# S5 stage of a hybrid decoder trunk: input columns in halves, chunk work in pairs, float32 gate products for four blocks

## The chip, the cores and the metric

The kernel runs on one core of a Trainium2 chip. The core has five engines that run at the same time, each with its own queue in order: TensorE (PE in the profile; its weight loads are shown as PEld), VectorE (DVE), ScalarE (ACT), GpSimd (POOL) and SyncE (SP), which here only issues transfers (DMA) between device memory and SBUF. PE writes its results to PSUM. The metric is device time in microseconds of one execution, the median of several runs. All times below are in microseconds where nothing else is said.

## What is computed

Two layers over 256 positions of width 1024; each has a SwiGLU block, a mixer and a second SwiGLU block, all with RMSNorm ahead and a residual sum behind. The mixer of layer 0 is S5, a diagonal state-space layer; that of layer 1 is block-sparse attention. Only S5 bears on this case:

```python
u = (h @ w_in).astype(f32)
...
    bu_re = jnp.einsum('bcgn,gpn->bcgp', u_c, bb_re)
    bu_im = jnp.einsum('bcgn,gpn->bcgp', u_c, bb_im)
    pr, pi, sr, si = lax.associative_scan(combine, (lam_re_b, lam_im_b, bu_re, bu_im), axis=1)
    ...
    y = jnp.einsum('bcgp,gnp->bcgn', st_re, c_re) - jnp.einsum('bcgp,gnp->bcgn', st_im, c_im)
...
y = ys.transpose(1, 0, 2, 3, 4).reshape(bsz, seq, S5_WIDTH) + d_skip.astype(f32) * u
g = jax.nn.gelu(y)
g = g * jax.nn.sigmoid(g @ w_glu.astype(f32))
return g.astype(h.dtype) @ w_out
```

An input product, a complex linear recurrence along the sequence, an output product per group, a gelu, a gate (product with `w_glu`, sigmoid, multiplication) and an output product. The weights of the three large products are 1024 x 1024 each.

## The kernel before

**Split products.** The large products keep nearly the precision of float32 with three fast products: each float32 operand is written as a high and a low part (type float32r), and high x high, high x low and low x high are summed in PSUM. Weights come from device memory as float32 in units of 1024 x 256 or 512 x 512 (`raw`, a ring of three buffers). A half of a unit is split by two instructions: ACT writes `whi` (line 84, or 90 with the norm's gains), DVE writes `wlo` (line 85 or 91). `Stream` keeps the order: `pump` splits the next half if a slot of the nine is free, `get` fetches a half and splits whatever is still missing, `release` gives the slot back after use, and once both halves of a unit are split its `raw` buffer is free and `dmas` issues the next load on SP. Order on every engine is the order in which the program is written out; an instruction that has to wait holds up all that stand behind it on its engine.

**S5.** The 1024 columns are eight blocks of 128. t is one of two halves of 128 positions. The steps, with the lines of the kernel before:

- `w_in` (lines 970 to 976): the input product for 512 columns and one t, 24 matmuls into a `pM` bank; ACT evicts it as `us` with the norm's factor (975), DVE transposes 32 x 32 pieces into `U` (976). Four such passes.
- `t1` (978 to 986), the chunk input of block b: 16 float32 matmuls of `U` with the table `TA` (loaded on SP, line 946). It needs `U` of the block's columns for both t.
- `rot` (988 to 1018), the rotation and scan of a block: on DVE two products `wv` of the PSUM result with the table `TE`, the sum and difference `zi`, two scans `zo`; then on POOL two products `pv` and the sum and difference `hr`. DVE also clears the first columns of `rh` and `zi` each time (993, 1004).
- `y_out` (1034 to 1051), the chunk output: 24 float32 matmuls of `U` and `hr` with the table `TB` (line 954), gelu on ACT (1047), two DVE transposes into `gs` (1050).
- `g_tr` (1053 to 1063): two PE transposes of `gs`; ACT writes the high part (1061), DVE the low part (1062), ACT a float32 copy `gf` (1063).
- `glu` (1065 to 1082): the block's share of the gate product, 24 matmuls of 256 columns into the four banks `pA`.
- `gate` (1084 to 1092): sigmoid on ACT (1087); on DVE the multiplication, the copy to the high part (1091) and the low part.
- `so`, the output product (through `bank_mm` and `mm3`, lines 397 to 399), and `boundary`, which adds the residual and prepares the next stage.

The order is written out by hand at the end of `s5`: rotations 0 to 2 hang as hooks in the third and fourth pass of the input product; after it come chunk outputs, gate products and the remaining chunk inputs by turns, one block at a time, with the gate product three blocks behind the chunk output.

## Time and profile before

| | us |
|---|---|
| median of 3 runs | 993.73 |
| lowest and highest | 992.82, 994.16 |
| profiled execution, its own time | 993.93 |
| its span in the trace | 991.9 |
| PE busy in the span | 973.8 |
| DVE busy | 703.3 |
| ACT busy | 559.2 |
| POOL busy | 192.1 |
| first input product of S5, start | 216.79 |
| first output product of S5, start | 298.30 |

How to read the views that follow. In a list of instructions by time, a row has the start from the begin of the span, the duration, the engine, the line of the kernel, the operation, what is written and read (tile names without numbers), shapes, the count of merged instructions, and in brackets how long the engine had been idle and whose end released it. Matmuls are pipelined: the distance between two starts is the price of one, not its duration. A float32 matmul appears as two records. In a row of groups stand the count, the busy time in all, the mean of one in nanoseconds, and the idle time before them with its releasers. In the view of stretches each row has the stretch, its length, the busy time of PE, PEld, DVE, ACT and POOL with counts, and then the clock granted to PE as a share of full speed, the share of the DMA engines' time and GB/s.

### The profile page before, as it was taken

The numbers are of one execution on the slowest core, as the hardware profiler recorded it, in microseconds if no ns is written. First come the engines' busy times: TensorE is split into PE (matmuls) and PEld (weight loads), VectorE is DVE, ScalarE is ACT, GpSimd is POOL, SyncE is SP. The second block draws the span as 40 slices with busy tenths as digits, with TensorE's granted clock in tenths as the row PEclk, the third lists the DMA queues.
The fourth block names the chain that finished last, engine by engine and source line by source line (L and its number), as shares of the span: only waits on it lengthen the run. The fifth ranks groups of instructions, "written<-read, shape, count | busy, mean of one in ns | idle before, by whom it ended". The sixth has DMA issues, their size and how long they took to land.

```text
span 991.9 us, 17175 instructions
## 1 busy us (share of the span) xinstructions
PE 973.8 (98%) x6695; PEld 866.0 (87%) x6695; DVE 703.3 (71%) x1148; ACT 559.2 (56%) x997; POOL 192.1 (19%) x361
## 2 busy tenths in 40 slices
PE   9999999999799999999999999999999999999998
PEld 7778888888687999999999999998888899999997
DVE  5799777768978776666667766665689667766662
ACT  6646666553255665555545555554898655655540
POOL 4882554414730100000010000000441010000000
PEclk9999999999999999999999999999999999999999
DMA  8978877886656565656536655554445446756531
GB/s 235 277 261 250 293 264 237 301 332 216 236 171 190 193 212 172 211 170 213 170 120 220 216 202 181 194 182 137 131 167 170 157 143 218 248 170 213 170 128 42
DMA packets 140000, 198.71 MB, mean 200 GB/s; under 512 B 18232, under 2 KB 111504, under 8 KB 139664
## 3 DMA queue, kind: packets, MB, share of 16 engines
q1 hardware_dynamic: 133808, 184.32, 56.2%
q0 software_dynamic: 5536, 12.71, 3.6%
q8 instruction: 52, 0.85, 0.4%
q10 hardware_dynamic: 576, 0.61, 0.3%
q14 instruction: 28, 0.23, 0.1%
HBM read 183.89 MB, written 13.66 MB: 199 GB/s over the span
## 4 chain that ended last, share of the span: by engine, by line
PE 84%; DVE 7%; POOL 3%; issue 2%; ACT 2%; DMA 1%; SPq 0%; ACTq 0%; DVEq 0%; POOLq 0%
PE pM L551 12%; PE pM L552 12%; PE pM L553 12%; PE pA L397 9%; PE pA L399 9%; PE pA L398 9%; PE pM L397 5%; PE pM L398 5%; PE pM L399 5%; DVE wlo L85 2%; DVE zo L1010 1%; POOL sc L685 1%; PE pR L331 1%; ACT whi L84 1%; PE pR L861 1%
## 5 line engine op out<-in xcount | busy, mean ns | idle before, releaser
L551 PE MATMUL pM<-xa,whi 128*128 128x256 f32 x1056 | 295.7, 280 | 0.0
L552 PE MATMUL pM<-xa,whi 128*128 128x256 f32 x1056 | 294.9, 279 | 0.0
L553 PE MATMUL pM<-xa,wlo 128*128 128x256 f32 x1056 | 294.7, 279 | 0.0
L91 DVE SCALAR_TENSOR_TENSOR wlo<-raw,gT,whi 128x512 fp32r<-128x512 f32 x328 | 228.2, 748 | 70.5 <-ACT whi L90 70.3
L85 DVE TENSOR_TENSOR wlo<-raw,whi 128x1024 fp32r<-128x1024 f32 (+1 forms) x157 | 191.4, 1234 | 55.6 <-ACT whi L84 54.7
L90 ACT ACTIVATE whi<-raw,gT 128x512 fp32r<-128x512 f32 x328 | 213.7, 711 | 19.6 <-PE pA L399 14.6
L552 PEld LDWEIGHTS pM<-xa,whi 128*128 128x128 f32 x1056 | 198.5, 188 | 2.6
L551 PEld LDWEIGHTS pM<-xa,whi 128*128 128x128 f32 x1056 | 198.5, 188 | 2.3
L553 PEld LDWEIGHTS pM<-xa,wlo 128*128 128x128 f32 x1056 | 198.5, 188 | 0.0
L84 ACT ACTIVATE whi<-raw 128x1024 fp32r<-128x1024 f32 (+1 forms) x157 | 161.1, 1049 | 29.1 <-PE pA L399 8.0
L397 PE MATMUL pA<-whi,ah 128*128 128x512 f32 x352 | 138.8, 394 | 0.0
L398 PE MATMUL pA<-wlo,ah 128*128 128x512 f32 x352 | 137.6, 391 | 0.0
L399 PE MATMUL pA<-whi,al 128*128 128x512 f32 x352 | 137.6, 391 | 0.0
L566 ACT ACTIVATE sg<-gr 128x256 f32<-128x256 f32 x66 | 27.6, 418 | 165.8 <-DVE gr L563 165.8
L397 PE MATMUL pM<-whi,xa 128*128 128x512 f32 x288 | 119.5, 415 | 0.0
L398 PE MATMUL pM<-wlo,xa 128*128 128x512 f32 x288 | 113.1, 393 | 0.1
L399 PE MATMUL pM<-whi,xa 128*128 128x512 f32 x288 | 112.7, 391 | 0.0
L346 POOL TENSOR_TENSOR ms<-ss 128x1 f32<-128x1 f32 x10 | 1.9, 193 | 472.1 <-ACT sq L343 472.1
L399 PEld LDWEIGHTS pA<-whi,al 128*128 128x128 f32 x352 | 66.1, 188 | 14.3
L397 PEld LDWEIGHTS pA<-whi,ah 128*128 128x128 f32 x352 | 66.1, 188 | 11.6
L398 PEld LDWEIGHTS pA<-wlo,ah 128*128 128x128 f32 x352 | 66.2, 188 | 11.3
L563 DVE TENSOR_TENSOR gr<-pM,rrow 128x512 f32<-128x512 f32 x66 | 45.5, 689 | 40.9 <-PE pM L553 40.8
(263 smaller groups left out, 1232.5 us busy)
## 6 DMA issues: line engine op xcount, KB each, us to landing
raw<-in_ffn_w_down_dram SPq DMA_DIRECT2D x44, 1024.0 KB, 5.2
raw<-in_ffn_w_gate_dram SPq DMA_DIRECT2D x80, 512.0 KB, 3.8
raw<-in_ffn_w_up_dram SPq DMA_DIRECT2D x80, 512.0 KB, 4.9
raw<-in_moba_w_qkv_dram SPq DMA_DIRECT2D x12, 1024.0 KB, 5.1
TB<-dB SPq DMA_DIRECT2D x8, 768.0 KB, 6.0
raw<-in_ffn_w_gate_dram SPq DMA_DIRECT2D x16, 256.0 KB, 4.2
raw<-in_ffn_w_up_dram SPq DMA_DIRECT2D x16, 256.0 KB, 4.7
dB<-tt POOLq DMA_DIRECT2D x16, 256.0 KB, 6.0
```

The lines of the kernel that those rows point to most:

```text
L84: nc.scalar.activation(hi[:, c], r[:, c], AF.Copy)
L85: nc.vector.tensor_tensor(lo[:, c], r[:, c], hi[:, c].bitcast(F32), op=OP.subtract)
L90: nc.scalar.activation(hi[:, c], r[:, c], AF.Identity, scale=g)
L91: nc.vector.scalar_tensor_tensor(lo[:, c], r[:, c], g, hi[:, c].bitcast(F32), op0=OP.mult, op1=OP.subtract)
L397: mm(o, xh, wh, start=start, stop=False)
L398: mm(o, xh, wl, start=False, stop=False)
L399: mm(o, xl, wh, start=False, stop=stop)
L551: mm(o, a, xh, start=k == 0 and i == 0, stop=False, skip_group_check=True)
L552: mm(o, a, xl, start=False, stop=False, skip_group_check=True)
L553: mm(o, b, xh, start=False, stop=k == 7, skip_group_check=True)
L563: V.tensor_tensor(gr, ps.rearrange("p (i c) -> p i c", i=2), Rr["row"][:, None, :].to_broadcast([128, 2, 256]), op=OP.mult)
L566: nc.scalar.activation(sg, gr[:, 0, :], AF.Silu)
```

## The change

It edits S5 and what `Stream` needs for it.

- The first 512 input columns are computed in two halves of 256, each for both t (four passes of 24 matmuls of 256 columns instead of two of 512); the second 512 as before. The first half's weights stay in their slots until the fourth pass.
- Chunk inputs go in pairs (`t1x2`), with the loads of two further tables behind them; chunk outputs go in pairs as well. The order at the end of `s5` is written anew: the pair 0, 1 and rotation 0 hang in the third pass, rotation 1 in the fourth, the pair 2, 3 and rotation 2 in the fifth (the first of 512 columns), rotation 3 and the chunk outputs 0 and 1 in the sixth.
- For blocks 0 to 3 (`WHOLE = 4`) the gate product is one float32 matmul instead of three split ones, read from `raw` and `gf` directly. These weights aren't split, and their `raw` buffer is freed when PE has used both halves. `g_tr` then makes no high and low part for these blocks.
- Weights are loaded in another order: three gate units, one output unit, the fourth gate unit, three output units. Where splits are pumped within the gate products is a table, `PUMPS`.
- `rh` and `zi` are cleared once, on POOL; `gs` is made by one DVE transpose instead of two; the gate's copy to the high part is on ACT instead of DVE; the tile of the gate's high and low parts starts at another offset.

```diff
-XO = {'f00': 124, 's5': 124, 'g': 8, 'f01': 80, 'f10': 8, 'moba': 124, 'f11': 8}
+XO = {'f00': 124, 's5': 124, 'g': 124, 'f01': 80, 'f10': 8, 'moba': 124, 'f11': 8}
...
-            self.halves += [(u, 0), (u, 1)]
+            if not units[u][3]:
+                self.halves += [(u, 0), (u, 1)]
...
-        for b in range(4):
-            add(("glu", b), ld_rows(s5_w_glu[0], b * 256))
-        for b in range(4):
-            add(("so", b), ld_rows(s5_w_out[0], b * 256))
+        for key in (('glu', 0), ('glu', 1), ('glu', 2), ('so', 0), ('glu', 3), ('so', 1), ('so', 2), ('so', 3)):
+            w = s5_w_glu if key[0] == "glu" else s5_w_out
+            add(key, ld_rows(w[0], key[1] * 256), whole=key[0] == "glu" and 2 * key[1] < WHOLE)
...
-        def w_in(nh, t, hooks, pumps=(1, 5)):
+        RH = [wp.tile([128, 4, 65], F32, name=f"rh{i}") for i in range(2)]
+        ZI = wp.tile([128, 2, 4, 65], F32, name="zi")
+        for a in RH:
+            P.memset(a[:, :, 0:1], 0.0)
+        P.memset(ZI[:, :, :, 0:1], 0.0)
+
+        def w_in(c0, n, t, hooks, last, pumps=(1, 5)):
...
+                mm3(ps[:, 0:n], X["h"][:, k, ts], X["l"][:, k, ts], wh[:, c:c + n], wl[:, c:c + n], k == 0, k == 7)
+                if k % 2:
+                    if k in pumps:
+                        st.pump()
+                    if last:
+                        st.release(u, (k % 4) // 2)
             us = wp.tile([128, 512], F32, name="us", bufs=1)
-            nc.scalar.activation(us, ps, AF.Identity, scale=Rr[t])
-            V.transpose(U[:, nh * 16:(nh + 1) * 16, t, :], us.rearrange("p (q c) -> p q c", c=32))
+            nc.scalar.activation(us[:, 0:n], ps[:, 0:n], AF.Identity, scale=Rr[t])
+            V.transpose(U[:, c0 // 32:(c0 + n) // 32, t, :], us[:, 0:n].rearrange("p (q c) -> p q c", c=32))
...
+        def t1x2(b):
+            for a in (b, b + 1):
+                t1(a)
+            for a in (b, b + 1):
+                if a + 3 < NB:
+                    ld_a(a + 3)
...
-            for t in range(2):
-                V.transpose(gs[:, t], yg[:, :, t, :])
+            V.transpose(gs, yg.rearrange("p q t c -> p t q c"))
...
-            nc.scalar.activation(GT["h"][:, b, :], ps[:, 0:256], AF.Copy)
-            V.tensor_tensor(GT["l"][:, b, :], ps[:, 0:256], GT["h"][:, b, :].bitcast(F32), op=OP.subtract)
+            if b >= WHOLE:
+                nc.scalar.activation(GT["h"][:, b, :], ps[:, 0:256], AF.Copy)
+                V.tensor_tensor(GT["l"][:, b, :], ps[:, 0:256], GT["h"][:, b, :].bitcast(F32), op=OP.subtract)
...
+                if b < WHOLE:
+                    mm(d, w[:, c], g, start=first, stop=last, skip_group_check=True)
...
-                if o == 7:
+                for _ in range(PUMPS.get((b, o), 0)):
+                    st.pump()
+                if o == 7 and b >= WHOLE:
                     st.release(u, b % 2)
-                if o == 3 and b < 5 or o == 7 and b in (3, 4) or o == 5 and b == 4:
-                    st.pump()
+                elif o == 7 and b % 2:
+                    st.free_raw(u)
...
-            V.tensor_copy(gh, g)
+            nc.scalar.activation(gh, g, AF.Copy)
...
+        PUMPS = {(1, 3): 1, (2, 3): 1, (4, 1): 1, (4, 5): 1, (5, 0): 1, (5, 2): 1, (5, 4): 1, (5, 6): 1}
+        w_in(0, 256, 0, entry_hooks("s5") if entry else {}, False)
+        w_in(0, 256, 1, {}, False, (1,))
+        w_in(256, 256, 0, {5: [lambda: t1x2(0), lambda: rot(0)]}, False, ())
+        w_in(256, 256, 1, {4: [lambda: rot(1)]}, True, (1,))
+        w_in(512, 512, 0, {2: [lambda: t1x2(2), lambda: rot(2)]}, False, ())
+        w_in(512, 512, 1, {1: [lambda: rot(3)], 6: [lambda: y_out(0), lambda: y_out(1)]}, True, ())
+        GT["h"], GT["l"] = home(xp, "g")
+        t1x2(4)
+        rot(4)
         g_tr(0)
+        glu(0)
+        rot(5)
+        g_tr(1)
         y_out(2)
+        y_out(3)
+        glu(1)
+        t1x2(6)
+        rot(6)
+        g_tr(2)
+        glu(2)
+        g_tr(3)
+        rot(7)
+        glu(3)
+        y_out(4)
+        y_out(5)
+        g_tr(4)
+        glu(4)
+        g_tr(5)
+        glu(5)
+        y_out(6)
+        y_out(7)
...
+        g_tr(6)
         g_tr(7)
-        st.pump(2)
         warm(AF.Sigmoid)
-        glu(5)
         for i in range(4):
             glu(6, (2 * i, 2 * i + 1))
             glu(7, (2 * i, 2 * i + 1))
```

64 lines of the change are left out of this document (23 added, 41 removed).

## The prediction

> **What bounds the kernel now.** I read the page first, then busy time by stretch for the S5 part, then the order of instructions on each engine there. The page's span and the chain that ended last:
>
> ```profile
> span 991.9 us, 17175 instructions
> PE 84%; DVE 7%; POOL 3%; issue 2%; ACT 2%; DMA 1%; SPq 0%; ACTq 0%; DVEq 0%; POOLq 0%
> ```
>
> TensorE (PE) carries the chain, so the change is worth what it does to PE's idle time and work. It touches S5 alone, whose stretch runs from the first input product to the first output product. The first and last row below are those two; the three between are PE's long waits (in brackets: idle before, and releaser).
>
> ```profile
> 216.79 0.48 PE L397 MATMUL pM<-whi,xa 128*128 128x512 f32 x1
> ...
> 252.64 0.69 PE L1059 MATMUL pR<-cst,gs 128*128 128x128 f32 x2 [3.97 <-DVE gs L1050]
> ...
> 271.39 0.44 PE L1059 MATMUL pR<-cst,gs 128*128 128x128 f32 x2 [2.28 <-ACT gf L1063]
> ...
> 278.34 0.44 PE L1059 MATMUL pR<-cst,gs 128*128 128x128 f32 x2 [1.95 <-ACT gf L1063]
> ...
> 298.30 0.47 PE L397 MATMUL pA<-whi,xa 128*128 128x512 f32 x1 [0.53 <-DVE xa L1091]
> ```
>
> The stretches around the waits (PE, PEld, DVE, ACT, POOL busy; then granted clock, DMA share, GB/s):
>
> ```profile
> 248.70:252.60 3.90, 0.00 (x0) 0.00 (x0) 3.88 (x6) 0.00 (x0) 2.54 (x4) 1.00 0.63 205
> 252.60:257.00 4.40, 4.36 (x70) 3.75 (x72) 3.83 (x11) 2.13 (x6) 4.03 (x4) 0.61 1.01 407
> ...
> 264.00:272.00 8.00, 5.72 (x102) 5.22 (x98) 7.24 (x13) 1.05 (x3) 6.30 (x6) 1.00 0.54 186
> 272.00:284.00 12.00, 10.05 (x166) 9.38 (x163) 9.19 (x18) 5.34 (x11) 8.39 (x8) 1.00 0.27 89
> ```
>
> While PE waits, VectorE (DVE) is busy: DVE's queue, in order, is what PE waits for. After the idle 3.97 the clock falls to 0.61 for 4.40, a loss of 4.40 x 0.39 = 1.7; after 2.28 and 1.95 it stays at 1.00. So S5 holds 3.97 + 2.28 + 1.95 + 0.53 = 8.7 of idle and 1.7 of slow clock: 10.4 to be won at most.
>
> **The change part by part.** PE prices, each from the distance between starts:
>
> ```profile
> 223.49 0.39 PE L397 MATMUL pM<-whi,xa 128*128 128x512 f32 x1
> ...
> 228.02 0.39 PE L399 MATMUL pM<-whi,xa 128*128 128x512 f32 x1
> ...
> 230.38 1.15 PE L985 MATMUL pA<-U,TA 128*64 128x64 f32 x32
> 231.46 0.50 PE L397 MATMUL pM<-whi,xa 128*128 128x512 f32 x1
> ...
> 244.50 0.34 PE L1043 MATMUL pR<-U,TB 128*64 128x64 f32 x4
> ...
> 247.52 1.15 PE L985 MATMUL pM<-U,TA 128*64 128x64 f32 x32
> ...
> 265.39 0.28 PE L1076 MATMUL pA<-xa,whi 128*128 128x256 f32 x1
> ...
> 267.75 0.28 PE L1078 MATMUL pA<-xa,wlo 128*128 128x256 f32 x1
> ```
>
> ```profile
> 768.36 0.60 PE L1213 MATMUL pA<-kT,qT 128*128 128x256 f32 x2
> 768.79 0.59 PE L1250 MATMUL pR<-pT,vs 128*128 128x256 f32 x2
> ```
>
> A split product of 512 columns takes 4.53/20 = 0.227, one of 256 columns 2.36/20 = 0.118, a float32 one of 256 columns (two records) 0.43, a block's chunk input 1.08, a chunk output (244.50 to 247.52 is two) 1.5.
>
> Input in halves: 96 x 0.118 replace 48 x 0.227: +0.4. Gate products of four blocks: 32 x 0.43 = 13.8 replace 96 x 0.118 = 11.3: +2.4. Chunk inputs in pairs: from 228.02 to 230.38 stand ten products and 0.1 more, the price of a switch; four fewer switches in and out save 0.8. Work in sum: +2.0.
>
> DVE and POOL prices:
>
> ```profile
> 224.42 2.72 DVE L91 SCALAR_TENSOR_TENSOR wlo<-raw,gT,whi 128x512 fp32r<-128x512 f32 x4
> 231.58 0.69 DVE L1005 TENSOR_TENSOR wv<-pA,TE 128x512 f32<-128x512 f32 x1 [0.15 <-PE pA L985]
> 233.58 1.28 DVE L1010 TENSOR_TENSOR_SCAN zo<-rh,zi 128x260 f32<-128x260 f32 x2
> 234.98 0.69 DVE L1005 TENSOR_TENSOR wv<-pA,TE 128x512 f32<-128x512 f32 x1
> 236.30 1.52 DVE L1007 TENSOR_TENSOR zi<-wv,wv 128x256 f32<-128x256 f32 x1
> 238.61 1.82 DVE L1010 TENSOR_TENSOR_SCAN zo<-rh,zi 128x260 f32<-128x260 f32 x2
> ```
>
> ```profile
> 235.00 1.29 POOL L1014 TENSOR_TENSOR pv<-zo,TE 128x512 f32<-128x512 f32 x1 [11.73 <-DVE zo L1010]
> 236.25 1.28 POOL L1015 TENSOR_TENSOR pv<-zo,TE 128x512 f32<-128x512 f32 x1
> 237.61 0.79 POOL L1016 TENSOR_TENSOR hr<-pv,pv 128x256 f32<-128x256 f32 x1
> 238.37 0.92 POOL L1017 TENSOR_TENSOR hr<-pv,pv 128x256 f32<-128x256 f32 x1
> ```
>
> The first rotation (231.58 to 234.86) takes 3.3 with POOL idle; the second (234.98 to 240.43) takes 5.4, its zi standing until POOL's pv ends: the two take turns on their SBUF operands, instruction by instruction. The wv products, which read PSUM, aren't slowed.
>
> ```profile
> L975 ACT ACTIVATE us<-pM,rr 128x512 f32<-128x512 f32 x4 | 2.8, 688 | 15.5 <-PE pM L399 11.9 <-issue 2.3 <-POOL rs_e L307 1.2
> L1063 ACT ACTIVATE gf<-pR 128x256 f32<-128x256 f32 x8 | 3.1, 384 | 20.0 <-DVE xa L1062 20.0
> L976 DVE STREAM_TRANSPOSE U<-us 128x512 f32<-128x512 f32 x4 | 2.8, 700 | 3.2 <-ACT us L975 3.2
> L1062 DVE TENSOR_TENSOR xa<-pR,xa 128x256 fp32r<-128x256 f32 x8 | 3.3, 410 | 0.7 <-ACT xa L1061 0.7
> ```
>
> *The new wait.* The built order puts on DVE: rotation 0, transpose of half two of t = 0, the pair of input-weight splits, rotation 1, transpose of half two of t = 1, rotation 2. PE's chunk input of block 2 reads that last transpose, and behind it on PE stand chunk input 3 and the whole second half of the input product. Count both from the start T of chunk input 0. PE: the pair 2.2, nine products 1.1, the pass 24 x 0.118 = 2.8, six products of 512 at 1.4, switches 0.4: at the wait by T + 7.9. DVE: 1.2 to the rotation (230.38 to 231.58), 3.3, transpose 0.35 (half of 0.70, an estimate), splits 2 x 0.68, rotation 1 at 3.3, transpose 0.35: T + 9.9 with POOL idle. But POOL's work for rotation 0 (about 4.3 from the four rows, 3.0 of it not beside wv) takes turns with just these splits and this rotation; before, it cost rotation 1 2.1. With what PE already needed for block 0 no reason excludes either end: PE idles 9.9 - 7.9 = 2.0 at the least, 2.0 + 3.0 = 5.0 at the most. I take 2.4 for the turns, between the 2.1 seen and the 3.0, since splits now stand in POOL's way as well as zi: an idle of 4.4. That is nearest to the row of 3.97, so the clock drop of 1.7 comes again.
>
> The Trainium skill (TensorE: Matmul & The Clock Gate, "What's actually happening") has the clock halve only after a whole idle window of about 3.4 us, and the windows run free of the kernel. By that an idle of 4.4 covers a whole window three times in ten (an estimate from that page), and the sum would then lose most of the 1.7. The trace agrees that a short idle costs no clock; where the border lies it leaves open, as one idle of 3.97 did drop it.
>
> *Waits that follow.* T itself: the eviction of half one of t = 1 now stands on ACT behind the split of the last input weights, whose load lands late:
>
> ```profile
> 209.49 0.38 SPq L185 DMA_DIRECT2D raw<-in_s_w_in_dram  x1
> raw<-in_s_w_in_dram SPq DMA_DIRECT2D x1, 1024.0 KB, 13.4
> ```
>
> ```profile
> 223.64 2.55 ACT L90 ACTIVATE whi<-raw,gT 128x512 fp32r<-128x512 f32 x4
> ```
>
> 209.5 + 13.4 = 222.9, then two ACT splits at 0.64, an eviction and a transpose of half size (0.35 each) and handovers: 225.4. PE has passed 63 products by 216.8 + 63 x 0.118 + 0.8 for the entering transposes = 225.0: 0.4. Before chunk input 4 PE waits for the last eviction 0.69 and transpose 0.70: 1.4. A gate product right behind its transpose waits for one ACT copy of 0.38 and handovers: 0.5 for blocks 0, 2, 3 (block 1 is covered by two chunk outputs): 1.5. Blocks 4 and 5 still wait for ACT 0.38 and DVE 0.41 one after the other, behind a gelu or two splits: 0.9 each, 1.8. At the end four splits of gate and output weights are pumped within block 5:
>
> ```profile
> 287.68 3.50 DVE L85 TENSOR_TENSOR wlo<-raw,whi 128x1024 fp32r<-128x1024 f32 x3 [0.43 <-ACT whi L84]
> ```
>
> 4 x 1.17 = 4.7 on DVE, begun 1.4 after the block's products, against 2.8 + 2 x 1.5 on PE; both last gelu transposes and their split stand behind them: 1.5 in all.
>
> New waits: 4.4 + 1.7 + 0.4 + 1.4 + 1.5 + 1.8 + 1.5 = 12.7. The sum: 12.7 + 2.0 - 10.4 = +4.3.
>
> Costed at nothing: three memsets on POOL, which has nothing else until rotation 0 but the two small norms; four result splits (0.41) and four weight splits (1.17) that DVE no longer has to make: what they can give is in the 10.4, all of which I credit. The gate's copies go to ACT: one handover more before the first output product, which waits 0.53 for that copy now; PE still has 36 x 0.118 = 4.2 of gate products to run while the first gate is made, and uncovered it costs about that 0.5 once more. The moved address of the gate tile adds no instruction. Chunk tables come in pairs, earlier than their use. Weights of blocks 0 to 3 hold their buffer until PE has used them, so the next loads wait for PE in SP's queue, with the last chunk table behind them: covered if it lands as usual, and a rival below.
>
> The profiled run took 993.93 (span 991.9 and 2.0 around it), 0.2 from the median 993.73. 993.7 + 4.3 = 998.0.
>
> **The rivals.** With S for the idle before chunk input 2, the change is S + (1.7 if the clock drops) - 1.8.
>
> *Not slower: turns with POOL cost nothing at this place.* Then S = 2.0, too short for a drop (2.28 wasn't enough): +0.2, 993.9, no change that could be told. For it: the input splits never ran beside pv in this trace, and rotation 1 could lag POOL and slip between. Against: zi at 1.52 and the scan at 1.82. It decides while S stays under some 2.3; above, each tenth counts fully and the clock comes on top.
>
> *The clock holds through the idle of 4.4:* nothing between 2.28 (held) and 3.97 (dropped) is measured, and one drop may have needed its place in time: 998.0 - 1.7 = 996.3. This is what the Trainium skill's page above would make of it seven times in ten.
>
> *Handovers hide too, faster:* S = 2.0 and of the later waits of 1.4 + 1.5 + 1.8 + 1.5 = 6.2 most, say 4.8, gone, since DVE has eight splits fewer in its queue: 993.9 - 4.8 = 989.1. Against: each of them is a read of what the step before has just made, with no other PE work queued between.
>
> *A late table:* the load for block 7 is issued behind an output-weight load that waits for the fourth gate block.
>
> ```profile
> TB<-dB SPq DMA_DIRECT2D x8, 768.0 KB, 6.0
> ```
>
> From its issue to its use PE has some 10; at 6.0 it is covered, at the 13.4 of the w_in load it is 3.4 late: 1001.4.
>
> **How the numbers follow.** Forecast 998.0, chance 0.45 (own range 996.3 to 1000); clock holds 0.13; POOL costs nothing 0.18; handovers hide 0.12; late table 0.12. Measurement tells 0.2% (2.0) from no change: faster below 991.7 is the handovers' case and a fifth of POOL's, 0.16; 991.7 to 995.7 the rest of POOL's and the low edge of the clock's, 0.19; slower 0.65. The range 991.5 to 1001.5 leaves the handovers' case and half of the late table outside.
>
> **What would show it.** Right: the chunk input of block 2 has an idle of 4 to 5 before it, ended by DVE's transpose U; the clock under 0.7 behind it; rotation 1 over 5; float32 gate products 0.43 apart; the first output product near 302.6. Wrong: S under 2.3, or the first output product before 298.3; a wait on DMA in S5 makes it the last rival.

## The result, and the profile after

The changed kernel takes 997.69 us in the median of 6 runs (996.67 to 998.29); the kernel before takes 993.64 beside it (992.82 to 994.16, 6 runs). The ratio is 1.0039 with a 95% interval of 1.0029 to 1.005: 0.4% slower. The prediction was 998.0. The profiled execution took 997.11, with a span of 995.2.

The page of the changed kernel, its span and the chain that ended last:

```profile
span 995.2 us, 17176 instructions
PE 84%; DVE 6%; POOL 5%; issue 2%; ACT 1%; DMA 1%; SPq 0%; POOLq 0%; ACTq 0%
```

PE still carries the chain with 84%; of the rest, DVE's share went from 7 to 6% and POOL's from 3 to 5%. The instructions of PE in S5 by time (start, duration, operation, in brackets the idle time before and what ended it); the first and last row are the first input and the first output product, as in the prediction:

```profile
216.61 0.36 PE L398 MATMUL pM<-whi,xa 128*128 128x256 f32 x1
...
225.47 2.09 PE L1004 MATMUL pA<-U,TA 128*64 128x64 f32 x64 [0.63 <-issue]
237.16 3.53 PE L1004 MATMUL pA<-U,TA 128*64 128x64 f32 x64 [4.17 <-DVE U L995]
255.17 2.08 PE L1004 MATMUL pM<-U,TA 128*64 128x64 f32 x64 [1.53 <-DVE U L995]
...
258.10 3.72 PE L1091 MATMUL pA<-gf,raw 128*128 128x256 f32 x16 [0.47 <-ACT gf L1072]
261.66 0.38 PE L1067 MATMUL pR<-cst,gs 128*128 128x128 f32 x2
...
283.42 0.38 PE L1093 MATMUL pA<-xa,whi 128*128 128x256 f32 x1 [0.47 <-ACT xa L1070]
...
287.54 0.38 PE L1093 MATMUL pA<-xa,whi 128*128 128x256 f32 x1 [0.47 <-ACT xa L1070]
288.51 0.39 PE L1094 MATMUL pA<-xa,whi 128*128 128x256 f32 x1 [0.59 <-DVE xa L1071]
...
294.89 0.44 PE L1067 MATMUL pR<-cst,gs 128*128 128x128 f32 x2 [0.47 <-DVE gs L1060]
...
302.31 0.39 PE L398 MATMUL pA<-whi,xa 128*128 128x512 f32 x1
```

S5, from the first input product to the first output product, takes 302.31 - 216.61 = 85.70, against 81.51 before: 4.19 more, which is the size of the difference between the medians (997.69 - 993.64 = 4.05). The spans of the two profiled executions differ by less, 995.2 - 991.9 = 3.3: 0.2 is won ahead of S5, and the output product behind it takes 16.36 to the next stage's first transpose instead of 17.07. The three long waits of before (3.97, 2.28, 1.95) are gone. In their place stands one of 4.17, in the middle of the input product, ahead of the chunk input of block 2, and then a row of short ones. The stretches of the long wait and behind it (busy time of PE, PEld, DVE, ACT, POOL; then granted clock, DMA share, GB/s):

```profile
233.00:237.16 4.16, 0.01 (x1) 0.01 (x1) 4.07 (x8) 0.00 (x0) 2.02 (x4) 0.98 0.61 171
237.16:241.60 4.44, 4.44 (x68) 4.25 (x69) 2.39 (x5) 0.00 (x0) 3.66 (x4) 0.64 0.67 214
```

PE does nothing for 4.16, DVE works through all of it, and behind it the clock is at 0.64 for 4.44: a further 4.44 x 0.36 = 1.6. The two chunk inputs that follow the wait take 3.53 for that reason; the pair ahead of it took 2.09. What DVE does in that time, and POOL beside it:

```profile
223.59 1.41 DVE L92 SCALAR_TENSOR_TENSOR wlo<-raw,gT,whi 128x512 fp32r<-128x512 f32 x2 [0.77 <-ACT whi L91]
...
230.20 3.37 DVE L92 SCALAR_TENSOR_TENSOR wlo<-raw,gT,whi 128x512 fp32r<-128x512 f32 x2
233.49 0.68 DVE L1028 TENSOR_TENSOR wv<-pA,TE 128x512 f32<-128x512 f32 x1
...
235.48 1.28 DVE L1033 TENSOR_TENSOR_SCAN zo<-rh,zi 128x260 f32<-128x260 f32 x2
236.68 0.42 DVE L995 STREAM_TRANSPOSE U<-us 128x256 f32<-128x256 f32 x1
```

```profile
230.02 1.30 POOL L1037 TENSOR_TENSOR pv<-zo,TE 128x512 f32<-128x512 f32 x1 [6.95 <-DVE zo L1033]
231.28 1.75 POOL L1038 TENSOR_TENSOR pv<-zo,TE 128x512 f32<-128x512 f32 x1
```

The last row of DVE is the transpose that PE waits for; rotation 1 (233.49 to 236.7) stands ahead of it, and ahead of that the pair of splits, which takes 3.37 beside POOL's two products for rotation 0. The pair of the same shape in the first row, ahead of POOL's products, took 1.41.

### The profile page after: what moved, and what is told of

It reads as the page before. It is cut to its first block, busy times and chain, and to the rows that moved or that the text cites. A ratio compares the mean times of both kernels' runs of the same rounds, so it can differ in the third digit from the quotient of the medians.

```text
span 995.2 us, 17176 instructions
## 1 busy us (share of the span) xinstructions
PE 975.2 (98%) x6711; PEld 868.3 (87%) x6711; DVE 689.3 (69%) x1114; ACT 557.6 (56%) x995; POOL 192.4 (19%) x364
## 4 chain that ended last, share of the span: by engine, by line
PE 84%; DVE 6%; POOL 5%; issue 2%; ACT 1%; DMA 1%; SPq 0%; POOLq 0%; ACTq 0%
PE pM L553 12%; PE pM L552 12%; PE pM L554 12%; PE pA L398 9%; PE pA L400 9%; PE pA L399 9%; PE pM L398 4%; PE pM L399 4%; PE pM L400 4%; DVE wlo L86 2%; PE pA L1091 1%; POOL sc L686 1%; POOL qrs L305 1%; PE pR L1054 1%; PE pR L332 1%
## 5 line engine op out<-in xcount | busy, mean ns | idle before, releaser
L86 DVE TENSOR_TENSOR wlo<-raw,whi 128x1024 fp32r<-128x1024 f32 (+1 forms) x153 | 184.9, 1223 | 55.7 <-ACT whi L85 54.4
L85 ACT ACTIVATE whi<-raw 128x1024 fp32r<-128x1024 f32 (+1 forms) x153 | 156.8, 1049 | 29.2 <-PE pA L400 7.8
L398 PE MATMUL pM<-whi,xa 128*128 128x512 f32 (+1 forms) x304 | 122.0, 401 | 0.0
L399 PE MATMUL pM<-wlo,xa 128*128 128x512 f32 (+1 forms) x304 | 115.7, 381 | 0.3 <-DVE wlo L92 0.2
L400 PE MATMUL pM<-whi,xa 128*128 128x512 f32 (+1 forms) x304 | 115.4, 380 | 0.0
L398 PEld LDWEIGHTS pA<-whi,ah 128*128 128x128 f32 x352 | 66.1, 188 | 11.6
```

Of the source, the lines that this page charges most:

```text
L85: nc.scalar.activation(hi[:, c], r[:, c], AF.Copy)
L86: nc.vector.tensor_tensor(lo[:, c], r[:, c], hi[:, c].bitcast(F32), op=OP.subtract)
L398: mm(o, xh, wh, start=start, stop=False)
L399: mm(o, xh, wl, start=False, stop=False)
L400: mm(o, xl, wh, start=False, stop=stop)
```

## Experiments

Times are medians; each ratio is to the kernel before, run beside it, with a 95% interval. "S5" is the stretch between the two products above, in the profiled execution of each kernel.

**Rotation 1 behind the transpose.** Is the 4.17 the loss, and is it rotation 1's place in DVE's queue?

```diff
-w_in(256, 256, 1, {4: [lambda: rot(1)]}, True, (1,))
-w_in(512, 512, 0, {2: [lambda: t1x2(2), lambda: rot(2)]}, False, ())
+w_in(256, 256, 1, {}, True, (1,))
+w_in(512, 512, 0, {0: [lambda: rot(1)], 2: [lambda: t1x2(2), lambda: rot(2)]}, False, ())
```

> The changed kernel with one move: rotation 1 is issued behind the eviction and transpose of half two of t = 1, so the transpose that the chunk input of block 2 waits for stands ahead of rotation 1 on DVE. Nothing else is changed. Theory (that wait is the loss, and its price is the idle of 4.17 plus the slow clock behind it): DVE is through with the two splits at about 233.6 and makes the transpose at 234.0, so the idle before the chunk input of block 2 falls from 4.17 to about 1.0, the granted clock behind it stays at 0.98 or more, and the time falls by 3.2 + 1.4 = 4.6, to about 993.1. Rival (the wait is only moved): rotation 2, chunk input 4 or the handovers of the gate products take back at least half of it: 995.5 or more, with an idle above 3 before chunk input 4. Rival (the loss is in the float32 gate products): no change, 997.5 or more.

Measured: 992.09, ratio 0.9988 (0.9979 to 0.9996). PE by time, then DVE by time:

```profile
232.79 2.08 PE L1004 MATMUL pA<-U,TA 128*64 128x64 f32 x64 [1.01 <-DVE U L995]
```

```profile
229.00 3.38 DVE L92 SCALAR_TENSOR_TENSOR wlo<-raw,gT,whi 128x512 fp32r<-128x512 f32 x2
232.30 0.43 DVE L995 STREAM_TRANSPOSE U<-us 128x256 f32<-128x256 f32 x1
```

The splits are as slow as in the changed kernel, the transpose follows them at once, the idle is 1.01 and the pair of chunk inputs runs in 2.08, at full clock. S5 takes 80.45, which is 5.25 less: 3.16 of idle, 1.45 in the pair by the clock, and the 0.63 ahead of the first chunk input, which isn't there in this execution. No later wait grew (before chunk input 4 it is 1.52). The 0.63 is most of the 1.0 by which the time is under the expectation, and it comes from when a load lands and not from the move (below, under the late load). Moving one call puts the changed kernel 0.1% below the kernel before, so the rest of the change is worth more than it costs.

**Split pair earlier.** What does POOL slow when the splits stand elsewhere?

```diff
-w_in(256, 256, 0, {5: [lambda: t1x2(0), lambda: rot(0)]}, False, ())
-w_in(256, 256, 1, {4: [lambda: rot(1)]}, True, (1,))
+w_in(256, 256, 0, {5: [lambda: t1x2(0), lambda: rot(0)]}, False, (1,))
+w_in(256, 256, 1, {4: [lambda: rot(1)]}, True, ())
```

> The changed kernel with one move: the last pair of input-weight splits is made one quarter of the input product earlier, so on DVE it stands ahead of rotation 0 (where DVE now idles 1.3) instead of between the transpose of half two of t = 0 and rotation 1. Rotation 1 still stands ahead of the transpose that the chunk input of block 2 waits for. Theory (POOL's work on rotation 0 takes turns with whatever DVE reads from SBUF beside it): the pair is back at 1.4 instead of 3.37, and rotation 1 takes 5.2 to 5.5 instead of 3.3, its first additive step and its scans stretched. The idle before the chunk input of block 2 falls by only 0.5 to 1.2, to 3.0 to 3.7; 996.5 to 997.2 if the clock still falls below 0.7 behind it, 995.0 to 995.8 if it holds. Rival (it was the place of the splits, not turns with POOL): the pair and rotation 1 both run at 1.4 and 3.3, the idle falls to about 1.4, and the time to 993.5.

Measured: 995.21, ratio 1.0019 (1.001 to 1.0029). DVE by time:

```profile
224.71 1.37 DVE L92 SCALAR_TENSOR_TENSOR wlo<-raw,gT,whi 128x512 fp32r<-128x512 f32 x2
...
229.62 0.65 DVE L1028 TENSOR_TENSOR wv<-pA,TE 128x512 f32<-128x512 f32 x1
...
230.90 1.37 DVE L1030 TENSOR_TENSOR zi<-wv,wv 128x256 f32<-128x256 f32 x1
232.19 0.94 DVE L1031 TENSOR_TENSOR zi<-wv,wv 128x256 f32<-128x256 f32 x1
233.06 1.80 DVE L1033 TENSOR_TENSOR_SCAN zo<-rh,zi 128x260 f32<-128x260 f32 x2
234.79 0.41 DVE L995 STREAM_TRANSPOSE U<-us 128x256 f32<-128x256 f32 x1
```

The pair is back at 1.37, and rotation 1 (229.62 to 234.8) takes 5.2 instead of 3.3: `zi` and the scans are stretched, `wv`, which reads PSUM, is not. So the price of POOL's turns goes with the place, as the theory had it, and the rival is out. The wait and what follows it, by stretch:

```profile
232.40:235.25 2.85, 0.02 (x1) 0.00 (x0) 2.80 (x4) 0.00 (x0) 1.57 (x3) 1.00 0.65 239
235.25:239.00 3.75, 3.75 (x72) 3.39 (x73) 2.51 (x4) 0.00 (x0) 3.67 (x4) 1.00 0.41 115
```

The idle is 2.83, a little under the 3.0 to 3.7 expected, and in this execution the clock held. It took 993.82, though, and the median of 995.21 is not its time: of the ten executions the four of 993.47 to 994.45 have a mean clock of 1.000, the six of 994.75 to 997.43 have 0.997 or 0.998. That the clock fell behind this idle in those six fits their times, but isn't shown, as only the one trace was kept. So the median, which falls into the expected 995.0 to 995.8 for a held clock, does so by luck, between two kinds of executions; those with the clock at 1.000 are below what was expected.

**Both moves.** The two edits above together:

```diff
-w_in(256, 256, 0, {5: [lambda: t1x2(0), lambda: rot(0)]}, False, ())
-w_in(256, 256, 1, {4: [lambda: rot(1)]}, True, (1,))
-w_in(512, 512, 0, {2: [lambda: t1x2(2), lambda: rot(2)]}, False, ())
+w_in(256, 256, 0, {5: [lambda: t1x2(0), lambda: rot(0)]}, False, (1,))
+w_in(256, 256, 1, {}, True, ())
+w_in(512, 512, 0, {0: [lambda: rot(1)], 2: [lambda: t1x2(2), lambda: rot(2)]}, False, ())
```

> Both moves: the pair of input-weight splits ahead of rotation 0, and rotation 1 behind the transpose of half two of t = 1. Theory: DVE has nothing between rotation 0 and that transpose, which is made as soon as ACT has evicted the half (about 232.6), before PE is at the chunk input of block 2 (233.0): the idle of 4.17 falls to under 0.3 and no clock drop stands behind it, 4.2 + 1.4 = 5.6 less, about 992.1, 1.0 under the run with rotation 1 moved alone. Rotation 1 then runs beside POOL's work for rotation 0 and takes 5 or more, at a place where PE doesn't wait for it. Rival (what is won here comes back): rotation 2 is later than before and chunk input 4 waits for DVE by more than 2 instead of 1.53; 994 or more.

Measured: 990.75, ratio 0.9974 (0.9964 to 0.9984). The pair of chunk inputs of blocks 2 and 3 by time shows no wait:

```profile
231.99 2.08 PE L1004 MATMUL pA<-U,TA 128*64 128x64 f32 x64
```

S5 takes 79.32: 6.38 less than in the changed kernel. The idle and the slow clock, 4.17 + 1.6 = 5.8, are what the moves won; the other 0.63, ahead of the first chunk input, is again absent in this execution. It is about half of the 1.35 by which the time is under the expectation; the rest isn't resolved. The wait before chunk input 4 stays at 1.52. One step of the expectation was wrong. Rotation 1 does not run beside POOL's work and does not take 5 or more. DVE by time:

```profile
231.25 0.45 DVE L995 STREAM_TRANSPOSE U<-us 128x256 f32<-128x256 f32 x1 [1.86 <-ACT us L994]
...
233.71 1.28 DVE L1033 TENSOR_TENSOR_SCAN zo<-rh,zi 128x260 f32<-128x260 f32 x2
...
238.06 2.31 DVE L1033 TENSOR_TENSOR_SCAN zo<-rh,zi 128x260 f32<-128x260 f32 x2
```

DVE stands idle for 1.86 ahead of the transpose, waiting for ACT's eviction, and POOL's two products for rotation 0 (229.13 to 231.67) pass in that time. Rotation 1 (231.61 to 234.99) then takes 3.4. It is rotation 2 (234.91 to 240.37) that runs beside POOL's next work and takes 5.5, and there PE doesn't wait.

**PE kept busy in the wait.** Fourteen products of a constant fill part of the idle; they change no output.

```diff
+def dummy():
+    ps = psR()
+    for _ in range(14):
+        mm(ps[:, 0:128], ones, ones, start=True, stop=True)
...
-w_in(512, 512, 0, {2: [lambda: t1x2(2), lambda: rot(2)]}, False, ())
+w_in(512, 512, 0, {2: [dummy, lambda: t1x2(2), lambda: rot(2)]}, False, ())
```

> The changed kernel with extra work alone: 14 float32 products of 128 columns of a constant, into a bank of PSUM that nobody reads, stand on PE right ahead of the chunk input of block 2, about 3.0 of PE time (half of 0.43 each) inside the idle of 4.17. The wait for DVE stays as it is: chunk input 2 starts at 237.2 as before, with an idle of about 1.2 ahead of it. Theory (the slow clock of 0.64 behind the wait follows from the idle itself): the clock behind it is 0.95 or more, the pair of chunk inputs takes 2.1 instead of 3.53, and the time falls by about 1.4, to 996.3, although PE has more work and the same wait. Rival (the drop belongs to this place in time, or to the start of chunk inputs, and not to the idle): the clock falls here as before, 997.5 to 998. Rival (PE work ahead of the wait delays something): slower than 998.

Measured: 995.53, ratio 1.0017 (1.0009 to 1.0026).

```profile
236.52 2.08 PE L1004 MATMUL pA<-U,TA 128*64 128x64 f32 x64 [1.05 <-DVE U L995]
```

The wait ends where it did (10.50 after the start of rotation 0's first DVE product, as in the changed kernel), and the pair runs at full clock. S5 takes 83.61: 2.09 less, 1.45 in the pair and 0.63 by the wait ahead of the first chunk input, absent here, which is most of the 0.8 under the expectation. The slow clock follows from PE's idleness, and has a price of its own.

**Split gate products again, twice.** The first version makes two of the four further weight splits that it needs inside the second half of the input product, and pumps the others, with one more, into blocks 0 and 3; the second makes all four inside the second half of the input product.

```diff
-    WHOLE = 4
+    WHOLE = 0
...
-w_in(512, 512, 0, {2: [lambda: t1x2(2), lambda: rot(2)]}, False, ())
+w_in(512, 512, 0, {2: [lambda: t1x2(2), lambda: rot(2)]}, False, (1, 5))
...
first version:
-PUMPS = {(1, 3): 1, (2, 3): 1, ...
+PUMPS = {(0, 3): 1, (1, 3): 1, (2, 3): 1, (3, 3): 1, (3, 7): 1, ...
second version:
-w_in(512, 512, 1, {...}, True, ())
+w_in(512, 512, 1, {...}, True, (1, 5))
```

> The changed kernel with the gate products of blocks 0 to 3 in split form again (96 products in place of 32 float32 ones), with the four weight splits that this needs pumped inside the second half of the input product and blocks 0 and 3. Nothing else is changed. Theory (the float32 products cost PE 0.61 a block, 2.4 in all, but spare DVE and ACT eight splits): PE's work falls by 2.4; each of blocks 0, 2 and 3 then waits for an ACT copy and a DVE subtraction in turn instead of one ACT copy, 0.5 to 0.6 more each, 1.5 to 1.8 in all; so 997.1, within 0.7 of the changed kernel. The idle before the chunk input of block 2 stays at 4.2 with the slow clock behind it. Rival (the float32 products are the loss): 995.3 or less, with no new wait. Rival (the relief of DVE is what the change lives on): chunk inputs 6 and the later transposes wait for DVE by 1 or more each, 999 or more.

> The changed kernel with the gate products of blocks 0 to 3 in split form, as in the run that came out at 1003.3, but with all four weight splits made inside the second half of the input product, so that none stands in the gate blocks that the changed kernel doesn't have there. Theory (what split products cost in this order is their second handover: the DVE subtraction of each block stands behind a rotation of 3.3 on DVE, and PE has nothing else queued): PE's work falls by 2.4; blocks 0 and 2 wait 1.5 longer each, block 1's or the chunk outputs behind it about 1.6, 4.6 in all, and the clock drops once more at one of them; 999.5 to 1001. Rival (the loss of that run was the place of the weight splits): waits of 0.5 to 0.6 a block, 996.5 to 997.5. Rival (float32 products are a loss by themselves): 995.3 or less.

Measured: the first 1003.3, ratio 1.0102 (1.0087 to 1.0117), the second 1000.15, ratio 1.0064 (1.0051 to 1.0077). The expectation for the first was wrong by 6: it had a block wait 0.5 to 0.6 longer for the DVE subtraction, as if DVE were free. In its profiled execution, the longest of its five (1006.61), blocks 0 and 2 wait 1.54 each for that subtraction, the clock is at 0.50 for 13.7 in all instead of 3.4, and chunk output 3 has a wait that no expectation had:

```profile
269.07 0.34 PE L1054 MATMUL pR<-U,TB 128*64 128x64 f32 x4 [3.71 <-ACT gf L1072]
```

Its bank is read last by the copy `gf` of block 1; on ACT that copy stands behind DVE's subtraction for block 1 (through at 268.6), and on DVE the subtraction stands behind a pumped weight split (2.07) and rotation 5. The second version was expected with DVE's queue counted, and came out inside its range, by other terms: blocks 0 and 2 wait 1.54 each and the clock falls once more, as expected, but the third wait of 1.6 didn't come. PE and DVE of the second version by time:

```profile
258.05 0.38 PE L1093 MATMUL pA<-xa,whi 128*128 128x256 f32 x1 [0.47 <-ACT xa L1070]
259.97 0.38 PE L1094 MATMUL pA<-xa,whi 128*128 128x256 f32 x1 [1.54 <-DVE xa L1071]
```

```profile
258.32 1.28 DVE L1033 TENSOR_TENSOR_SCAN zo<-rh,zi 128x260 f32<-128x260 f32 x2
259.52 0.40 DVE L1071 TENSOR_TENSOR xa<-pR,xa 128x256 fp32r<-128x256 f32 x1
```

PE waits for the low part `xa`, which DVE makes only when the rotation ahead of it in its queue is through. A float32 block needs no DVE step between its transposes and its products, only ACT's copy (0.47 of wait). S5 takes 305.24 - 216.44 = 88.80 with split products and well placed weight splits, 3.1 more than with float32, though PE has 2.4 less to do. Of the 3.1, 1.7 is the second fall of the clock and 0.4 the late load (0.99 instead of 0.63). By the medians split products cost 2.5 (1000.15 - 997.69). In this order the float32 products are a gain.

**All eight blocks in float32.** The doubled edit:

```diff
-    WHOLE = 4
+    WHOLE = 8
...
-PUMPS = {(1, 3): 1, (2, 3): 1, (4, 1): 1, (4, 5): 1, (5, 0): 1, (5, 2): 1, (5, 4): 1, (5, 6): 1}
+PUMPS = {(4, 1): 1, (4, 5): 1, (5, 0): 1, (5, 2): 1}
```

> The changed kernel with the gate products of all eight blocks in float32 (256 fewer split products' worth: 32 float32 ones in place of 96 split ones for blocks 4 to 7), so the edit is doubled; the four weight splits and four result splits of blocks 4 to 7 fall away. Theory (each block costs PE 0.61 more and gives back what its split handover costs): PE +2.4; the waits before blocks 4 and 5 (0.47 + 0.47 + 0.59) become one copy of 0.47 each and the two of 0.47 and 0.52 at the end go, since only two splits stand ahead of the last gelu transposes: -1.6; so the first output product about 0.8 later than in the changed kernel, 998.5. The splits of the following stage come in another order, so the place of the first output product tells more than the whole time. Rival (float32 products are free beside the waits): no later than in the changed kernel. Rival (they are the loss): 2.4 later.

Measured: 997.79, ratio 1.0044 (1.0032 to 1.0057). The first output product starts at 302.17, S5 takes 86.00: 0.3 more than in the changed kernel, where 0.8 was expected and the rivals had 0 and 2.4. For blocks 4 to 7, where DVE has no rotation ahead, more float32 is about even.

**Two splits out of the tail.**

```diff
-PUMPS = {..., (5, 0): 1, (5, 2): 1, (5, 4): 1, (5, 6): 1}
+PUMPS = {..., (5, 0): 1, (5, 2): 1, (6, 1): 1, (6, 3): 1}
```

> The changed kernel with two of the four splits that are pumped within gate block 5 (those of the second pair of output weights) moved behind the last two gelu transposes, into block 6. Theory (the four splits in DVE's queue hold up the last two gelu transposes): the waits of 0.47 and 0.52 before the last two transposes on PE go, and the first output product starts 1.0 earlier: 996.7. Rival (the splits now hold up the first two gates, and the output product waits for them): the two waits go, but one of 0.5 or more stands before the first output product, 997.2 or more. Nothing ahead of block 5 changes.

Measured: 999.42, ratio 1.0054 (1.0042 to 1.0067): the rival by its time, in part by its waits. PE by time:

```profile
294.80 0.44 PE L1067 MATMUL pR<-cst,gs 128*128 128x128 f32 x2 [0.59 <-DVE gs L1060]
...
301.68 0.50 PE L398 MATMUL pA<-whi,xa 128*128 128x512 f32 x1 [0.31 <-ACT xa L1110]
...
305.64 0.50 PE L398 MATMUL pA<-whi,xa 128*128 128x512 f32 x1 [0.68 <-ACT sg L1106]
307.63 0.50 PE L398 MATMUL pA<-whi,xa 128*128 128x512 f32 x1 [0.33 <-ACT sg L1106]
```

Only one of the two transposes got rid of its wait (the second is held by its gelu, made one after the other), and the wait before the first output product is 0.31, where the rival had 0.5 or more. The splits now hold up the sigmoids, and PE waits 0.31, 0.68 and 0.33: the later ones because the output product's third and fourth bank is the gate's, which the sigmoid has still to read. S5 takes 85.60, 0.1 less than in the changed kernel, and the two waits behind its end are 1.0 more; the rest of the 1.7 between the medians isn't resolved.

**A reordered S5, in four steps.** The first has both moves of the split pair and rotation 1, and further:

```diff
-(('glu', 0), ('glu', 1), ('glu', 2), ('so', 0), ('glu', 3), ('so', 1), ...)
+(('glu', 0), ('glu', 1), ('glu', 2), ('glu', 3), ('so', 0), ('so', 1), ...)
...
-w_in(512, 512, 1, {1: [...], 6: [lambda: y_out(0), lambda: y_out(1)]}, True, ())
+w_in(512, 512, 1, {1: [...], 6: [lambda: y_out(0), lambda: y_out(1)], 7: [lambda: g_tr(0)]}, True, ())
...
+glu(0); t1x2(4); rot(4); rot(5); g_tr(1); y_out(2); y_out(3); glu(1)
+t1x2(6); rot(6); g_tr(2); g_tr(3); glu(2); rot(7); y_out(4); y_out(5); glu(3)
+g_tr(4); g_tr(5); glu(4); y_out(6); y_out(7); glu(5, range(0, 5)); g_tr(6); g_tr(7); glu(5, range(5, 8))
```

with the output weights' pumps at (5, 5), (5, 7), (6, 1) and (6, 3).

> A version meant to beat both kernels. It has both moves of the third experiment (split pair ahead of rotation 0, rotation 1 behind the transpose of half two of t = 1); further, the gelu transposes of block 0 stand inside the last eighth of the input product and gate block 0 ahead of the chunk input of block 4; the transposes of blocks 2 and 3 stand together ahead of gate block 2, those of blocks 4 and 5 ahead of gate block 4, those of blocks 6 and 7 inside gate block 5, with chunk outputs 4 and 5 ahead of gate block 3 and 6 and 7 ahead of gate block 5; the weights of gate blocks 6 and 7 are loaded ahead of the first output weights, and the output weights are split behind the last gelu transposes. Theory (the waits left in S5 are handovers ACT to PE and DVE to PE with no other PE work queued between): against the third experiment the 1.52 before chunk input 4, three of 0.47 before float32 gate blocks, 0.47 + 0.47 + 0.59 in blocks 4 and 5 and 0.47 + 0.52 at the end go, 5.4 in all; 990.75 - 5.4 = 985.4, with a range of 984.5 to 987.5. Rival (the time comes back as waits for chunk outputs that are now asked for earlier, or for the later output weights): 989 or more, with waits on POOL hr or on DMA.

Measured: 991.23, ratio 0.9975 (0.9965 to 0.9985), 5.8 above the expectation and no better than both moves alone. S5 does get shorter (78.01), but with a wait at its end:

```profile
294.73 0.50 PE L398 MATMUL pA<-whi,xa 128*128 128x512 f32 x1 [2.22 <-ACT xa L1110]
```

```profile
292.50:294.70 2.20, 0.00 (x1) 0.00 (x0) 1.51 (x2) 0.79 (x3) 0.00 (x0) 1.00 0.80 283
294.70:296.00 1.30, 1.27 (x3) 0.80 (x4) 1.04 (x2) 1.30 (x2) 0.00 (x0) 0.77 0.69 284
296.00:298.00 2.00, 2.00 (x6) 1.58 (x5) 1.48 (x2) 0.59 (x2) 0.00 (x0) 0.50 0.04 6
```

Gate 0 stands behind three weight splits on ACT and DVE, and on ACT behind the load of the sigmoid's table (1.28) as well; PE idles 2.22, and the clock falls to 0.50 behind it. Two waits of 1.00 and 0.52 for the transposes of blocks 4 and 5 stand behind rotation 7 on DVE.

The second step puts rotation 7 behind chunk outputs 4 and 5, loads the sigmoid's table right behind the last gelu, and splits the second pair of output weights only behind gate 1:

```diff
-rot(7); y_out(4); y_out(5); glu(3)
+y_out(4); y_out(5); rot(7); glu(3)
...
-y_out(6); y_out(7); glu(5, range(0, 5))
+y_out(6); y_out(7); warm(AF.Sigmoid); glu(5, range(0, 5))
...
-PUMPS = {..., (5, 5): 1, (5, 7): 1, (6, 1): 1, (6, 3): 1}
+PUMPS = {..., (5, 5): 1, (5, 7): 1}
...
     gate(i)
+    if i == 1:
+        st.pump(2)
```

> The reordered version with its three remaining waits taken out: rotation 7 behind chunk outputs 4 and 5, so that DVE makes the gelu transposes of blocks 4 and 5 ahead of it; the sigmoid table loaded right behind the last gelu; the first output weights split inside gate block 5 and the second pair only behind gate 1, so that no split stands ahead of gates 0 and 1. Theory (the splits in the queues of ACT and DVE ahead of gate 0 made the 2.22 before the first output product, rotation 7 made the 1.00 and 0.52 before the transposes of blocks 4 and 5, and the slow clock of 0.50 for 3.4 behind the 2.22 goes with it): 2.2 + 1.5 + 1.5 less than the reordered version's 991.2, about 986.0, range 985 to 988. Rival (chunk outputs 6 and 7 then wait for POOL, whose work for rotation 7 now starts 3 later): a wait of 2 or more on hr before them, 988 or more. Rival (the second output weights come late): a wait before the fifth group of output products, 988 or more.

Measured: 988.93, ratio 0.9951 (0.9938 to 0.9963): the fastest of all, 0.5% below the kernel before, yet 2.9 above the expectation. S5 takes 74.98, and the clock is 1.00 throughout. What is left:

```profile
225.68 2.09 PE L1004 MATMUL pA<-U,TA 128*64 128x64 f32 x64 [1.28 <-issue]
...
295.52 0.50 PE L398 MATMUL pA<-whi,xa 128*128 128x512 f32 x1 [1.09 <-ACT sg L1106]
...
298.24 0.50 PE L398 MATMUL pA<-whi,xa 128*128 128x512 f32 x1 [1.06 <-ACT sg L1106]
```

The first is the late load of the last input weights (ACT's split waited for it to 223.06, with the eviction behind it). The other two are neither of the rivals: they are the gate's banks again, as in the tail experiment, with two splits ahead of gates 2 and 3.

The front of the reordering alone, on top of both moves, with everything from gate block 2 on as in the changed kernel:

```diff
-w_in(512, 512, 1, {1: [...], 6: [lambda: y_out(0), lambda: y_out(1)]}, True, ())
-t1x2(4); rot(4); g_tr(0); glu(0); rot(5); g_tr(1)
+w_in(512, 512, 1, {1: [...], 6: [lambda: y_out(0), lambda: y_out(1)], 7: [lambda: g_tr(0)]}, True, ())
+glu(0); t1x2(4); rot(4); rot(5); g_tr(1)
...
-g_tr(2); glu(2); g_tr(3); rot(7); glu(3)
+g_tr(2); g_tr(3); glu(2); rot(7); glu(3)
```

> The third experiment's version (both moves of split pair and rotation 1) with the front of the reordering alone: transposes of block 0 inside the last eighth of the input product, gate block 0 ahead of chunk input 4, transposes of blocks 2 and 3 together ahead of gate block 2. Everything from gate block 2 on is as in the changed kernel. Theory: the 1.52 before chunk input 4 goes and two of the three waits of 0.47 before float32 gate blocks, 2.3 in all less than 990.75: 988.4. Rival (the transposes of blocks 4 and 5 then wait for DVE, which is not made faster): 989.5 or more, with waits of 0.5 to 1.5 on gs there.

Measured: 989.55, ratio 0.9957 (0.9944 to 0.9971), at the border of theory and rival: S5 is 77.89, 1.4 less than with the two moves and not 2.3, since a wait of 0.61 on `gs` now stands before the transposes of block 4, and 0.77 ahead of the first chunk input, where the execution with the two moves had none.

The last step, on top of the second, makes each sigmoid right behind its gate products, and puts both splits of the last input weights behind the eviction (`gate_s` is the sigmoid, `gate` the rest):

```diff
-w_in(0, 256, 1, {}, False, (1,))
-w_in(256, 256, 0, {5: [lambda: t1x2(0), lambda: rot(0)]}, False, (1,))
+w_in(0, 256, 1, {}, False, ())
+w_in(256, 256, 0, {5: [lambda: t1x2(0), lambda: rot(0)]}, False, (1, 3))
...
-    gate(i)
-    if i == 1:
-        st.pump(2)
+    gate_s(i)
+    if i:
+        gate(i - 1) if i < 3 else st.pump(2)
+gate(2)
+gate(3)
```

> The second reordered version with its two largest remaining waits taken out. The split of the last input weights, whose load lands at 222.9 to 223.1, stands on ACT behind the eviction of half one of t = 1 and no longer ahead of it. The four sigmoids each follow their gate products at once, one ahead of the rest of the gate before, and the second pair of output weights is split behind the last sigmoid and gate 1. Theory (the 1.28 before the first chunk input is the late load passed on by ACT's order; the 1.09 and 1.06 inside the output product are its banks three and four, which the sigmoids of gates 2 and 3 still had to read): all three go, 3.4 less than 988.9, about 985.5, range 984.8 to 987. Rival (rotation 0 now stands behind two more splits on DVE and the chunk input of block 2 waits again): a wait of 1 or more there, 987 or more. Rival (the second output weights come too late for the fifth group of output products): a wait of 1 or more there.

Measured: 990.51 (987.9 to 991.62), ratio 0.9964 (0.9953 to 0.9976). The three waits are gone and S5 is the shortest, 74.04, but the time is not better. PE waits at the next stage instead, by time and by stretch:

```profile
309.57 0.66 PE L332 MATMUL pR<-cst,h 128*128 128x128 f32 x4 [2.01 <-DVE h L370]
```

```profile
307.60:309.60 2.00, 0.03 (x1) 0.03 (x1) 2.00 (x4) 0.14 (x1) 0.00 (x0) 1.00 0.98 323
```

PE is through with the output product earlier than DVE with its queue of weight splits, and the residual `h` stands behind them. The profiled execution is the fastest of the six (987.9), with a mean clock of 0.999; the three slowest, 991.22 to 991.62, have mean clocks of 0.996 to 0.998. That the clock falls behind this 2.01 in those executions fits their difference; it isn't shown, as there is no trace of them.

## Why the prediction was right, point by point

| term | predicted | in the trace after |
|---|---|---|
| idle and slow clock of before, all won back | 10.4 | 10.4 (none of the four waits is left) |
| wait for the late load (T) | 0.4 | 0.63 |
| idle before chunk input 2 (S) | 4.4 | 4.17 |
| slow clock behind it | 1.7 | 1.6 |
| before chunk input 4 | 1.4 | 1.53 |
| three float32 blocks behind their copy | 1.5 | 3 x 0.47 = 1.41 |
| blocks 4 and 5 | 1.8 | 0.47 + 0.47 + 0.59 = 1.53 |
| last gelu transposes | 1.5 | 0.47 + 0.52 = 0.99 |
| more work on PE | 2.0 | 4.19 - 11.86 + 10.43 = 2.76, by difference |
| sum | +4.3 | +4.19 |

- **The bound.** That the change is worth what it does to PE in S5 held to within 0.9: S5 grew by 4.19, the spans of the same two executions differ by 3.3, and the 0.7 won in the output product is no term of the prediction. That the medians differ by 4.05, so near to 4.19, is in part luck.
- **The new wait.** Its place, its cause (the transpose of half two of t = 1 behind rotation 1 on DVE), its size and its end were right. The size came out by two errors that offset each other: counted from the start T of chunk input 0, PE stood at the wait at T + 7.5 instead of T + 7.9, and DVE's transpose ended at T + 11.6 instead of T + 12.3. The experiment with rotation 1 moved shows the cause: 3.16 of the idle and all of the slow clock go with that one call.
- **Where POOL's turns fall.** This step was right in size and wrong in place. The prediction asked for rotation 1 over 5; it took 3.3. POOL's products for rotation 0 fell on the pair of splits instead: 3.37 - 1.41 = 2.0, against 2.4 taken. Both stand ahead of the same transpose, so PE saw the same wait. With the splits out of the way the turns did fall on rotation 1, with 5.2, and with both moves on rotation 2, with 5.5. The Trainium skill (SBUF — State Buffer, "Who interferes with whom") says that a DVE instruction with two SBUF inputs and a GpSimd instruction that reads SBUF exclude each other for a whole instruction; the rows agree, down to `wv`, which reads PSUM and kept its 0.65.
- **The clock.** It fell, so the rival with the clock held (996.3) is out for this kernel. The prediction took the fall from the nearest row, the idle of 3.97, and had no reason beyond that; the last section has one. The run with PE kept busy shows that this loss is the idle's: 1.45 in the pair of chunk inputs.
- **Late load.** The wait for the last input weights came, with 0.63. It is 0 to 1.28 in the profiled executions of the experiments, whose front is much the same, so this term belongs to the load's landing and not to the order: in the changed kernel ACT's split of these weights waits for the load until 222.84, with rotation 1 moved it starts at 221.39 and has no such wait.
- **More work.** Short by 0.76. A float32 block takes 261.66 - 258.10 = 3.56 to the next transpose, 0.12 over its eight products at 0.43, which makes 0.5 over four blocks; the rest lies in gaps that no row names.
- **The two last waits** were sized too high (1.8 and 1.5 for 1.53 and 0.99), which makes up for the work by chance.
- **The rivals.** POOL costing nothing (S = 2.0) is out by the 3.37. Handovers hidden: none was, but the reordered versions show that they can be. A late table for block 7: no wait on DMA stands in S5.

The prediction priced the float32 products as work alone, +2.4. That isn't wrong as a term, since the relief of DVE stands elsewhere in its sum, but the better of the two runs with split products shows what they bring in this order: 2.5 by the medians.

## What to carry to other kernels

Ask of every instruction that another engine waits for what stands ahead of it in its own queue: here one rotation ahead of a 0.42 transpose cost 4.8 (3.2 of idle and 1.6 of slow clock), and moving that call turned a loss of 0.4% into a gain of 0.1%, with the split pair moved too 0.3%. A slower form on the bounding engine (float32 products) can win if it takes out a handover through a queue that is full. When a wait is taken out near the end of a stage, look for who is late next before counting it: the tail experiment and three steps of the reordering lost theirs to a sigmoid, a bank or a residual that stood behind the moved work.

## What the hardware showed beside

The clock falls after shorter idles than one would read from the long ones. All seven idles of 3.71 to 4.19 were followed by a slow clock (one in the kernel before, one in the changed kernel, five in the experiments); of the shorter ones 2.28 and 1.95 (kernel before), 2.83 (split pair earlier) and 2.01 (last step) were not, but 2.22 was (first reordered version, 0.50 for 3.4), and so were two of the four of 1.54 in the versions with split gate products, all four with a wait of 0.47 and 0.4 of work ahead of them. So between 1.5 and 2.9 the length of the idle doesn't decide alone.

What decides can be worked out from the granted clock in narrow stretches. Each time the clock fell in S5 it stood at 0.50 for 3.41 or for twice that, 6.83. Within one execution the edges lie whole steps of 3.413 apart: in the kernel before it fell at 252.65 and again, near the end of the span, at 989.93, which is 216 steps later; in the changed kernel at 236.98 and 994.74, 222 steps. Between two edges lies a window. In the fourteen profiled executions, each cut into its own windows, some 3800 in all, the clock fell behind every window in which PE was idle for 1.88 or more, and held behind every one with 1.79 or less (windows already at 0.50 left out). The 2.83 of the split pair was cut by an edge into 1.43 and 1.41; the 2.22 of the first reordered version lay whole in one window (stretches as above, PE's busy time first, the clock third from the end):

```profile
230.44:233.85 3.41, 1.98 (x12) 1.38 (x10) 3.38 (x4) 0.78 (x2) 3.20 (x4) 1.00 0.89 330
233.85:237.26 3.41, 2.00 (x64) 1.95 (x64) 2.16 (x5) 0.00 (x0) 2.26 (x2) 1.00 0.16 56
```

```profile
291.98:295.39 3.41, 1.19 (x7) 0.62 (x5) 2.51 (x3) 2.00 (x4) 0.00 (x0) 1.00 0.91 288
295.39:298.81 3.42, 3.42 (x9) 2.71 (x9) 2.46 (x5) 1.83 (x4) 0.00 (x0) 0.50 0.24 64
```

By these figures a single idle under 1.8 is safe, one over about 3.8 leaves 1.88 in a window wherever the edge falls, so behind the 4.17 the clock had to fall, and between the two it is the place of the edges in that execution that decides. This is an inference from these traces; no run was made to test it.

The Trainium skill (TensorE: Matmul & The Clock Gate, "What's actually happening") has a free-running window and a drop after one idle window of about 3.4. The window, its length and that it runs free of the kernel agree with these rows; that the whole of it has to be idle does not, as in seven of the ten falls in S5 PE was idle for 1.88 to 3.01 of the 3.41.
